# Chunked recurrence in seventeen steps, value sums on VectorE, and another split of the weight sums

## The chip, the cores and the metric

The kernel runs on one core of a Trainium2 chip. The metric is the device time of one execution in microseconds, the median of several runs. One execution was also profiled; its rows say how long each engine worked and what it waited for. The engines are TensorE (PE in the rows; PEld are its weight loads), VectorE (DVE), ScalarE (ACT), GpSimd (POOL) and SyncE (SP); SP and POOL issue the DMAs.

## The reference, cut to what matters

The reference is a trunk of two layers on 1024 rows of 1024 numbers, all float32. Layer 0 mixes rows with a gated linear recurrence of eight heads of 128 columns, layer 1 with a convolution module; each is followed by a squared-ReLU MLP of width 4096 and by layer normalisations. What the change touches is the recurrence and, through their weights, the value projection and the second matrices of both MLPs:

```python
proj = h @ w_in                       # columns [q | forget | value | output gate]
f = lb + (1 - lb) * sigmoid(fz);  k = 1 - f;  log_f = log(max(f, 1e-6))
...
def step(S, inp):                     # chunks of C rows, b = cumsum of log f within a chunk
    scores = einsum('bhtd,bhsd,bhtsd->bhts', qc, kc, decay)
    o = einsum('bhts,bhsv->bhtv', scores, vc) + einsum('bhtd,bhdv->bhtv', qc * exp(bc), S)
    S = exp(b_last) * S + einsum('bhsd,bhsv->bhdv', kc * exp(b_last - bc), vc)
...
o = o * rsqrt(mean(o^2) + 1e-6) * norm_g * silu(g);  mix = o @ w_out
...
ff = square(relu(x @ ffn_w1)) @ ffn_w2
```

## The kernel before, in words

**Products.** Every matrix product is split by a scheme of seven products over the four quadrants of its operands (numbered 1 to 7) in place of eight, and every operand is cut into two reduced-precision parts: ScalarE casts the high part and VectorE subtracts it for the low part (`cut`), and three multiplications stand for one. Products 5, 6 and 7 need sums of quadrants, which have to be made before they are cut. Products 1, 5 and 6 are copied out of PSUM by ScalarE, and later products are added to or subtracted from these copies (`v_out`).

**The value projection** is the first stage. `v_products(i, jobs)` issues product i in four pieces of 12 multiplications, and behind each piece its output copy, one job of the list and a tick of a clock that counts products. The order is 1, 2, 5, 6, 7, 3, 4. The inputs' quadrants (`x00`, `x01` ...) are combined on VectorE. Of the weights' quadrants a0 to a3, VectorE makes a2 + a3 (product 5) and a0 + a2 + a3 (product 6). The sums a0 + a2 (product 7) and a0 + a1 + a2 + a3 (product 3) are made in DRAM by `value_sums`: SP copies a0 and a1 into a DRAM tile `vsum`, POOL's DMAs add a2 and a3 and then the one half to the other, and `sum_v` loads both sums on SP.

**The pairs' stage.** Twelve pairs (a head's query and forget columns, or the output gates of two heads) follow, with seven products each of 12 multiplications. Between them the recurrences of the heads are woven in. `recurrence(h)` is a generator, and each `yield` ends a step. `slot()` is called at every third multiplication (four times in a product); each time `pace` is added to a sum, and a step is taken when it reaches one. Two heads may be under way together: the next starts when the first is at step `LAG`, and the steps alternate so that the lead stays near `LAG`. A head goes like this:

- On VectorE, F is written from the forget gate, `total(n)` multiplies neighbouring decay factors to products over 2n rows, and `scale(n)` multiplies queries and keys of blocks of n rows by them (n = 1, 2, 4 ... 64). `qk`, `T` and `F` in the rows are these.
- On TensorE, score products for blocks of 8 rows, the 4-wide ones (from `kd`, through a reciprocal), and those for 16, 32 and 64 write `level_ps`, two PSUM banks. `put(1)`, `put(0)` and `put(2)` copy them by mask (a predicated copy on VectorE) into the score buffer A (`at`), of which there are two, used in turn.
- Keys are transposed on TensorE and copied by ScalarE (`kt`).
- Then come eight chunks of 128 rows, one in a step. Each has a score product with the values and, but for the first, a product of the queries with the state; up to the seventh it also has a state product (`kt` with the values) into one PSUM slot, out of which VectorE writes the new state, decayed, into one of two buffers. After the fourth and the eighth chunk `settle` normalises half of the result into the head's F tile, and `give` transposes it, scales it and stores it by SP (`od <- f`). F has one buffer.

That makes 22 steps in a head. The gating with the output gates follows by loads and stores of its own (`gate_out`).

**Sums for the MLPs' second matrices.** `block_sums` makes, for one of 8 blocks of each of the two layers, the sums of weight quadrants in DRAM: two copies of 1 MB on SP and three accumulating DMAs on POOL, spread over ticks when a gap is given. There are 16 sets. Ten are issued in the pairs' stage (one in every eight products, not in the last pair), four in the first MLP's up stage, behind its blocks 1, 3, 5 and 7 counted from 0, and two in the convolution module.

**The rest.** Output projection and normalisation, first MLP up (`x1f`, `fw` in the rows) and down (`dw`, `dh`), convolution module, second MLP. No line of these differs but for the place of the sums.

**Who sets the order.** The instructions of TensorE, POOL and SP run in the order of the program text. Those of VectorE and ScalarE do so only until the end of the value projection; after that, a planner that simulates the kernel sets their order when it is built (a helper records most instructions, so that the rows show its line L173). An engine takes its instructions in order, so one that waits holds all behind it.

Of the kernel before, what the change touches and what calls it, by code (L numbers as in the profile page):

```python
# [15 lines left out]
P = 128  # L16
# [3 lines left out]
H = 8  # L20
# [217 lines left out]
def body(ctx, tc, d, out):  # L238
# [24 lines left out]
    def run(kb, n, size):  # L263
        return [kb + i * size for i in range(n)]
# [82 lines left out]
    x00, x10, x01, x11, t6 = [view(kb, (4, HT), F32, "xr") for kb in run(112, 5, 8)]  # L347
    a0, a1, a2, a3, s7 = [view(kb, (2, 1024), F32, "vr") for kb in run(152, 5, 8)]
    vd = [[dram.tile([P, NTB, HT], F32, name=f"vd{m}{n}") for n in range(2)] for m in range(2)]
# [15 lines left out]

    def value_sums(t, w, gap):

        def flat(x):
            return x.rearrange("a p n -> p a n")

        nc.sync.dma_start(out=flat(t), in_=flat(w)[:, 0:2])
        later(gap, lambda: nc.gpsimd.dma_start(out=flat(t), in_=flat(w)[:, 2:4], accum_op=ALU.add))
        later(2 * gap, lambda: nc.gpsimd.dma_start(out=flat(t)[:, 1], in_=flat(t)[:, 0], accum_op=ALU.add, max_dma_last_dim=4096))

# [101 lines left out]
    nc.sync.dma_start(out=par, in_=d["par"])  # L476
    vsum = dram.tile([2, 2, P, 1024], F32, name="vsum")
    for j in range(2):
        value_sums(vsum[:, j], d["wv"][:, j], 4)
    make_identity(nc, ident)  # L480
# [12 lines left out]
    def sum_v(out, i):  # L493
        for j in range(2):
            nc.sync.dma_start(out=out[:, j], in_=vsum[i, j])

# [11 lines left out]
    for k in range(4):  # L508
        if k < 3:
            diff(x00, x00, x01, (k + 1,))  # L510
        cut_x(5, x00, (k,))
    add_v(a2, a2, a3)
    for t in range(NTB):
        v_out(1, t)
    cut_v(5, a2)

# [11 lines left out]

    v_products(2, [lambda: x6(0, 1), lambda: x6(2, 3), lambda: add_v(a0, a2, a0), lambda: cut_v(6, a0)])
    outs_v(5)  # L530
    assert not waiting
    sum_v(s7, 0)
    sum_v(a1, 1)
    lg = par[:, LB : LB + H]
# [11 lines left out]

    v_products(5, [lambda: x7(0, 1), lambda: x7(2, 3)])
    cut_v(7, s7)
    x4(0, 1, 2, 3)
# [42 lines left out]
    level_ps, out_ps = (banks[:, k : k + 2].rearrange("p k (a b) -> p (k a) b", b=P) for k in (3, 5))  # L592
    state_ps = banks[:, 7, :P]
    count = {"at": 0}
    qk, gates, vts = {}, {}, {}
# [12 lines left out]
    def recurrence(h):  # L608
# [35 lines left out]
        yield  # L644
        scale(1)
        grow(2)
        yield
# [9 lines left out]
        yield  # L657
        A = at_[count["at"] % 2]
        count["at"] += 1
        levels(K, Q)  # L660
# [55 lines left out]
        if h == H - 1:  # L716
            assert (h - 1, 1) in done
            load_values(2 * h + 1, F[:, HT:].rearrange("p (a b) -> p a b", a=NTB))
        for c in range(2 * NTB):
            vc = vts[2 * h + c // NTB][:, c % NTB]  # L720
            if state is None:
                tensor.matmul(out_ps[:, c, :], A[:, c, :], vc, start=True, stop=True)
            else:
                tensor.matmul(out_ps[:, c, :], A[:, c, :], vc, start=True, stop=False)
                tensor.matmul(out_ps[:, c, :], Q[:, c * P : (c + 1) * P], state, start=False, stop=True)
            if c < nk:
                tensor.matmul(state_ps, kt[:, c, :], vc, start=True, stop=True)
                new = p1("state")
                if state is None:
# [12 lines left out]
        yield  # L742
        give(1)
# [63 lines left out]
    recs, active, done, pace, alone = [], [], set(), [0.0, 0.0], [False]  # L807
    LAG = 12

# [65 lines left out]
    def tail(i):  # L875
        if i == 6:
            wb_raw.append(raws((112, 116)))
            wb.ahead(1)
        elif i == 5:
            oT.extend([half_x(0, "oT"), half_x(32, "oT")])  # L880
        elif i == 7:
            assert not any(a[0] == H - 2 and a[2] < 21 for a in active)
            wb.ahead(3)
            back.append(ring(run(64, 8, 2), wide_t, "back"))
            assert len(stored) == 2 * H - 4
            gated(0, range(H - 2))
        elif i == 3:
            for half in range(2):
                u, g = back[0](), gates.pop((H - 2, half))
                nc.sync.dma_start(out=u, in_=od[H - 2][half])  # L890
                mul(u, u, g)
                into(half, H - 2, u)
        elif i == 4:
            wb.ahead(4)
            wa_raw.append(raws((80, 84)))
            wa.ahead(4)
# [7 lines left out]
    for _ in range(5):  # L904
# [8 lines left out]
        {  # L913
            "qk": ((2, 2 * HT), 3), "kd": ((2, 2 * HT), 1), "at": (chunks, 2), "f": (two_t, 1), "T": (two_t, 1), "kt": (chunks, 1), "t": (wide_t, 4),
            "sq": (wide_t, 2), "u": (wide_t, 2), "mask": ((3, P), 1), "rt": ((2 * P,), 1), "state": ((P,), 2), "dec": ((2 * NTB,), 2),
        },
    )
    vs = ring((124, 126), rows, "v")
    mask = p1("mask")
    at_ = [p1("at") for _ in range(2)]  # L920
    nc.sync.dma_start(out=mask, in_=d["mask"])
    for t in at_:
        nc.gpsimd.memset(t, 0.0)
# [381 lines left out]
    for c in range(NFC):  # L1305
        for i in ORDER[2 if c < 2 else 0 :]:
# [341 lines left out]
```

## Time and profile before

| | us |
|---|---|
| three runs | 2181.7, 2185.71, 2176.25 |
| median | 2181.7 |
| profiled execution | 2177.8 |
| its span in the profile | 2176.0 |
| TensorE busy in it (97%) | 2101.8 |
| VectorE busy (66%) | 1443.3 |
| ScalarE busy (48%) | 1040.8 |
| GpSimd busy (17%) | 380.7 |

The span runs from the first to the last recorded instruction; 1.8 us of the execution lie outside it. Over the span the DMA engines moved 515.95 MB, 237 GB/s in the mean, and the mean granted clock of TensorE was 0.992 of full speed. In the rows of waits, `X a L1 <- Y b L2: t, n, m` says that engine X, about to write a, waited for engine Y's work on b: t us in all, n times, the longest m. In the rows of the timeline a line is a run of like instructions: start, duration, engine, line, operation, out <- in, and in brackets how long the engine stood before it and for whom. In the rows of windows the columns are the window, its length, the engine's busy time with the number of instructions, the granted clock (behind TensorE's column alone, or behind all engines'), the DMA engines' busy share and GB/s.

### The profile page before, as it was taken

The page shows a single profiled execution, that of the slowest core. Times are in us where ns is not written, and L with a number is a line of the kernel's source. Part 1 is how long each engine was busy: PE and PEld are TensorE (multiplying, and loading weights), DVE is VectorE, ACT ScalarE, POOL GpSimd, SP SyncE. Part 2 cuts the span into 40 slices and gives each one's busy share as a digit, 9 for nine tenths or more (in the row PEclk, how much of TensorE's full clock was granted, in tenths as well). Part 3 has the DMA queues.
Part 4 walks back from the last instruction along what each step waited for, and adds up shares of the span by engine and source line. Part 5 has one row for each costly group of instructions (what it writes and reads, how often), then busy time and mean ns, then how long its engine had stood idle before and what let it go on. Part 6 is the DMA issues. An engine that isn't in the chain of part 4 may idle for free.

```text
span 2176.0 us, 27188 instructions
## 1 busy us (share of the span) xinstructions
PE 2101.8 (97%) x10056; PEld 1739.6 (80%) x10056; DVE 1443.3 (66%) x1886; ACT 1040.8 (48%) x1599; POOL 380.7 (17%) x349
## 2 busy tenths in 40 slices
PE   8889998999999999999999999999999999999998
PEld 6777776777888877878888888888878888888887
DVE  7587777867776665655566699789727444554446
ACT  4445454443255554634444577558552443443333
POOL 0001111111100000100001399279311000000002
PEclk9999999999999999999999999999999999999999
DMA  9566766676249988998998855665495888866652
GB/s 284 173 144 169 214 159 190 170 191 230 81 141 320 300 307 268 322 406 301 341 334 307 324 200 193 218 228 184 152 296 220 313 325 312 315 197 196 193 165 100
DMA packets 176318, 515.95 MB, mean 237 GB/s; under 512 B 16697, under 2 KB 45625, under 8 KB 175161
## 3 DMA queue, kind: packets, MB, share of 16 engines
q1 hardware_dynamic: 166392, 477.52, 62.0%
q0 software_dynamic: 9792, 36.70, 9.4%
q8 instruction: 78, 1.28, 0.2%
q14 instruction: 56, 0.45, 0.1%
HBM read 384.66 MB, written 201.85 MB: 270 GB/s over the span
## 4 chain that ended last, share of the span: by engine, by line
PE 71%; DMA 13%; DVE 7%; issue 3%; ACT 3%; POOL 3%; SPq 0%; DVEq 0%; POOLq 0%; ACTq 0%
PE ps L173 71%; POOL cb L173 2%; DMA next<-in_wpw_dram 2%; DVE qk L173 2%; DMA dh<-hf 1%; DMA wa<-ready 1%; DMA vsum<-in_wv_dram 1%; DMA hf<-ht 1%; DMA od<-f 1%; DMA y<-kept 1%; DMA hf<-hr 1%; DVE at L173 1%; DMA raw<-in_w1q_dram 1%; DVE fs L173 0%; DMA ready<-spare 0%
## 5 line engine op out<-in xcount | busy, mean ns | idle before, releaser
L173 PE MATMUL ps<-dw,dh 128*128 128x512 f32 x2688 | 612.9, 390 | 4.7 <-ACT dh L70 4.1
L173 PEld LDWEIGHTS ps<-dw,dh 128*128 128x128 f32 x2688 | 505.4, 188 | 110.2 <-ACT dh L70 4.6
L173 PE MATMUL ps<-x1f,fw 128*128 128x512 f32 x1344 | 309.7, 391 | 7.8 <-ACT c L1151 6.1
L173 PEld LDWEIGHTS ps<-x1f,fw 128*128 128x128 f32 x1344 | 251.1, 188 | 62.1 <-ACT c L1151 8.4
L173 PE MATMUL ps<-xa,wa 128*128 128x512 f32 x1152 | 268.8, 392 | 0.0
L173 PE MATMUL ps<-xf,fs 128*128 128x512 f32 x1008 | 265.7, 407 | 0.0
L173 PEld LDWEIGHTS ps<-xa,wa 128*128 128x128 f32 x1152 | 214.3, 188 | 43.3
L173 POOL TENSOR_TENSOR cb<-cb,prod 128x512 f32<-128x512 f32 x176 | 234.3, 1340 | 15.6 <-ACT prod L1416 4.7
L173 DVE TENSOR_TENSOR dw<-dr,dw 128x1024 fp32r<-128x1024 f32 x112 | 136.6, 1223 | 124.8 <-ACT dw L70 124.4
L173 DVE TENSOR_TENSOR dh<-dh 128x1024 fp32r<-128x1024 f32 x112 | 136.6, 1223 | 112.5 <-ACT dh L70 112.5
L173 PEld LDWEIGHTS ps<-xf,fs 128*128 128x128 f32 x1008 | 183.3, 191 | 34.3
L173 DVE SCALAR_TENSOR_TENSOR ps<-u,par,ps 128x512 f32<-128x512 f32 x288 | 199.1, 750 | 11.7 <-ACT ps L1428 10.2
L70 ACT CAST dh<-dh 128x1024 fp32r<-128x1024 f32 x112 | 117.1, 1050 | 150.0 <-DMA dh<-hf 149.2
L70 ACT CAST dw<-dr 128x1024 fp32r<-128x1024 f32 x112 | 117.4, 1052 | 141.4 <-PE ps L173 123.1
L173 PE MATMUL ps<-xc,wa 128*128 128x512 f32 x768 | 174.4, 389 | 0.0
L173 PEld LDWEIGHTS ps<-xc,wa 128*128 128x128 f32 x768 | 144.1, 188 | 29.8
L487 POOL TENSOR_TENSOR mv<-mv,nhalf 128x1 f32<-128x1 f32 x32 | 46.5, 1453 | 675.9 <-DVE mv L173 675.9
L1416 ACT ACTIVATE prod<-u,par 128x512 f32<-128x512 f32 x176 | 126.3, 723 | 61.6 <-POOL cb L173 60.3
L173 DVE TENSOR_TENSOR wa<-raw,wa 128x1024 fp32r<-128x1024 f32 x55 | 71.4, 1299 | 71.8 <-ACT wa L70 71.7
L70 ACT CAST wa<-raw 128x1024 fp32r<-128x1024 f32 x55 | 57.7, 1050 | 121.7 <-PE ps L173 106.0
L173 PE MATMUL ps<-vw,xf 128*128 128x512 f32 x336 | 82.5, 410 | 13.9 <-ACT vo L438 8.6
L1279 POOL COPY next<-ss 128x1 f32<-128x1 f32 x37 | 18.9, 510 | 414.3 <-DVE spare L173 271.6
(198 smaller groups left out, 2692.1 us busy)
## 6 DMA issues: line engine op xcount, KB each, us to landing
wa<-ready SPq DMA_DIRECT2D x122, 512.0 KB, 4.7
dh<-hf SPq DMA_DIRECT2D x112, 512.0 KB, 4.2
ready<-spare SPq DMA_DIRECT2D x74, 512.0 KB, 5.6
sum_w<-in_w_dram SPq DMA_DIRECT2D x32, 1024.0 KB, 7.5
dr<-sum_w SPq DMA_DIRECT2D x64, 512.0 KB, 4.7
raw<-in_w_dram SPq DMA_DIRECT2D x51, 512.0 KB, 5.5
dr<-in_w_dram SPq DMA_DIRECT2D x48, 512.0 KB, 6.4
raw<-in_w1q_dram SPq DMA_DIRECT2D x36, 512.0 KB, 5.1
```

The source lines that it names most:

```text
L70: self.nc.scalar.copy(out=slot[:, 0, c], in_=raw[:, c])
L173: return op(*args, **kw)
L487: nc.gpsimd.tensor_tensor(out=dst, in0=src, in1=nhalf[:, :n], op=ALU.pow)
L1279: nc.gpsimd.tensor_copy(out=raw[:, :1], in_=now)
L1416: nc.scalar.activation(tp, u[:, k : k + HT], AF.Copy, scale=tap(j, k))
```

## The change

**Value sums.** `value_sums`, `sum_v` and the DRAM tile go. VectorE makes all sums: s5 = a2 + a3 (product 5), s5 + a0 (product 6), a2 + a0 (product 7) and a1 + s5 (product 3), the last two as jobs behind the third and fourth piece of product 5. a2 is kept for that, and the fifth buffer holds s5 in place of the loaded sum.

**The recurrence** has 17 steps in place of 22. `scale(1)` and `grow(2)` become two steps. The state bank has four slots; `outer` issues the state products of four (then three) chunks together with the state updates behind them, and `attend` issues the products of four chunks with scores and states. One step holds `outer` of chunks 0 to 3, one `attend` of 0 to 3 with `outer` of 4 to 6, one `attend` of 4 to 7, then one `give` each. There are eight state buffers in place of two, and one score buffer in place of two. `LAG` is 9 instead of 12, and `pace` 0.54 and 0.5 instead of 0.74 and 0.66.

**Sums for the second matrices.** One set comes in every six products in the pairs' stage until four are left, which makes twelve; two come in the first up stage, behind blocks 0 and 2; two in the convolution module, as before.

```diff
-    a0, a1, a2, a3, s7 = [view(kb, (2, 1024), F32, "vr") for kb in run(152, 5, 8)]
+    a0, a1, a2, a3, s5 = [view(kb, (2, 1024), F32, "vr") for kb in run(152, 5, 8)]
-    def value_sums(t, w, gap):
...
-    vsum = dram.tile([2, 2, P, 1024], F32, name="vsum")
-    for j in range(2):
-        value_sums(vsum[:, j], d["wv"][:, j], 4)
...
-    add_v(a2, a2, a3)
+    add_v(s5, a2, a3)
     for t in range(NTB):
         v_out(1, t)
-    cut_v(5, a2)
+    cut_v(5, s5)
...
-    v_products(2, [lambda: x6(0, 1), lambda: x6(2, 3), lambda: add_v(a0, a2, a0), lambda: cut_v(6, a0)])
+    v_products(2, [lambda: x6(0, 1), lambda: x6(2, 3), lambda: add_v(s5, s5, a0), lambda: cut_v(6, s5)])
     outs_v(5)
-    assert not waiting
-    sum_v(s7, 0)
-    sum_v(a1, 1)
...
-    v_products(5, [lambda: x7(0, 1), lambda: x7(2, 3)])
-    cut_v(7, s7)
+    v_products(5, [lambda: x7(0, 1), lambda: x7(2, 3), lambda: add_v(a2, a2, a0), lambda: add_v(a1, a1, s5)])
+    cut_v(7, a2)
...
-    state_ps = banks[:, 7, :P]
-    count = {"at": 0}
+    state_ps = banks[:, 7].rearrange("p (a b) -> p a b", b=P)
...
         scale(1)
+        yield
         grow(2)
...
-        A = at_[count["at"] % 2]
-        count["at"] += 1
...
-        for c in range(2 * NTB):
-            vc = vts[2 * h + c // NTB][:, c % NTB]
-            if state is None:
-                tensor.matmul(out_ps[:, c, :], A[:, c, :], vc, start=True, stop=True)
-            else:
-                tensor.matmul(out_ps[:, c, :], A[:, c, :], vc, start=True, stop=False)
-                tensor.matmul(out_ps[:, c, :], Q[:, c * P : (c + 1) * P], state, start=False, stop=True)
-            if c < nk:
-                tensor.matmul(state_ps, kt[:, c, :], vc, start=True, stop=True)
+        def outer(cs):
+            for c in cs:
+                tensor.matmul(state_ps[:, c % NTB], kt[:, c, :], values(c), start=True, stop=True)
+            for c in cs:
                 new = p1("state")
-                if state is None:
-                    vector.tensor_copy(out=new, in_=state_ps)
+                if c == 0:
+                    vector.tensor_copy(out=new, in_=state_ps[:, 0])
                 else:
-                    vector.scalar_tensor_tensor(out=new, in0=state, scalar=dec[:, c : c + 1], in1=state_ps, op0=ALU.mult, op1=ALU.add)
-                state = new
-            if c % NTB == NTB - 1:
-                settle(c // NTB)
-                if h < H - 2:
-                    load_values(2 * h + 2 + c // NTB)
-            if c == 6:
-                give(0)
-            yield
-        yield
+                    vector.scalar_tensor_tensor(out=new, in0=states[c], scalar=dec[:, c : c + 1], in1=state_ps[:, c % NTB], op0=ALU.mult, op1=ALU.add)
+                states.append(new)
+
+        def attend(cs):
+            for c in cs:
+                tensor.matmul(out_ps[:, c, :], A[:, c, :], values(c), start=True, stop=c == 0)
+                if c:
+                    tensor.matmul(out_ps[:, c, :], Q[:, c * P : (c + 1) * P], states[c], start=False, stop=True)
+
+        outer(range(NTB))
+        yield
+        attend(range(NTB))
+        outer(range(NTB, nk))
+        settle(0)
+        yield
+        attend(range(NTB, 2 * NTB))
+        settle(1)
+        if h < H - 2:
+            for half in range(2):
+                load_values(2 * h + 2 + half)
+        yield
+        give(0)
         yield
         give(1)
...
-    LAG = 12
+    LAG = 9
...
-            "qk": ((2, 2 * HT), 3), ..., "at": (chunks, 2), ..., "state": ((P,), 2), "dec": ((2 * NTB,), 2),
+            "qk": ((2, 2 * HT), 3), ..., "at": (chunks, 1), ..., "state": ((P,), 8), "dec": ((2 * NTB,), 2),
...
-        pace[1] = 0.0 if p == 0 else 0.74 if p < 3 else 0.66
+        pace[1] = 0.0 if p == 0 else 0.54 if p < 3 else 0.5
...
-            if (7 * p + ORDER.index(i)) % 8 == 1 and p < len(PAIRS) - 1:
+            if (7 * p + ORDER.index(i)) % 6 == 1 and len(to_sum) > 4:
                 block_sums(*to_sum.pop(0), gap=12)
...
-        if c in (1, 3, 5, 7):
+        if c in (0, 2):
             block_sums(*to_sum.pop(0), f[:2, 1, :1].bitcast(F32))
```

More of the change, by code (lines that the diff above doesn't have):

```diff
@@ L364, in tick @@
                 job()
-    def value_sums(t, w, gap):
[L368 to L373, printed above, removed]
     sums = {}
@@ L491, in add_v @@
             vector.tensor_tensor(out=out[:, j], in0=x[:, j], in1=y[:, j], op=ALU.add)
-    def sum_v(out, i):
-        for j in range(2):
-            nc.sync.dma_start(out=out[:, j], in_=vsum[i, j])
     def diff(out, x, y, ks):
@@ L716, in recurrence @@
         if h == H - 1:
-            assert (h - 1, 1) in done
             load_values(2 * h + 1, F[:, HT:].rearrange("p (a b) -> p a b", a=NTB))
-        for c in range(2 * NTB):
-            vc = vts[2 * h + c // NTB][:, c % NTB]
-            if state is None:
-                tensor.matmul(out_ps[:, c, :], A[:, c, :], vc, start=True, stop=True)
-            else:
-                tensor.matmul(out_ps[:, c, :], A[:, c, :], vc, start=True, stop=False)
-                tensor.matmul(out_ps[:, c, :], Q[:, c * P : (c + 1) * P], state, start=False, stop=True)
-            if c < nk:
-                tensor.matmul(state_ps, kt[:, c, :], vc, start=True, stop=True)
+        states = [None]
@@ L728, in recurrence, with values @@
+        def values(c):
+            return vts[2 * h + c // NTB][:, c % NTB]
+        def outer(cs):
+            for c in cs:
+                tensor.matmul(state_ps[:, c % NTB], kt[:, c, :], values(c), start=True, stop=True)
+            for c in cs:
                 new = p1("state")
-                if state is None:
-                    vector.tensor_copy(out=new, in_=state_ps)
-                else:
-                    vector.scalar_tensor_tensor(out=new, in0=state, scalar=dec[:, c : c + 1], in1=state_ps, op0=ALU.mult, op1=ALU.add)
@@ L881, in tail @@
         elif i == 7:
-            assert not any(a[0] == H - 2 and a[2] < 21 for a in active)
+            assert not any(a[0] == H - 2 and a[2] < 15 for a in active)
             wb.ahead(3)
@@ L913, in body @@
         {
-            "qk": ((2, 2 * HT), 3), "kd": ((2, 2 * HT), 1), "at": (chunks, 2), "f": (two_t, 1), "T": (two_t, 1), "kt": (chunks, 1), "t": (wide_t, 4),
-            "sq": (wide_t, 2), "u": (wide_t, 2), "mask": ((3, P), 1), "rt": ((2 * P,), 1), "state": ((P,), 2), "dec": ((2 * NTB,), 2),
+            "qk": ((2, 2 * HT), 3), "kd": ((2, 2 * HT), 1), "at": (chunks, 1), "f": (two_t, 1), "T": (two_t, 1), "kt": (chunks, 1), "t": (wide_t, 4),
+            "sq": (wide_t, 2), "u": (wide_t, 2), "mask": ((3, P), 1), "rt": ((2 * P,), 1), "state": ((P,), 8), "dec": ((2 * NTB,), 2),
         },
@@ L919, in body @@
     mask = p1("mask")
-    at_ = [p1("at") for _ in range(2)]
+    A = p1("at")
     nc.sync.dma_start(out=mask, in_=d["mask"])
-    for t in at_:
-        nc.gpsimd.memset(t, 0.0)
+    nc.gpsimd.memset(A, 0.0)
     for i in range(2):
```

## The prediction

> **What bounds the kernel now.** I read the page first, then TensorE's waits in two parts of the span, its clock in short windows, and the timeline around each long wait.
>
> ```profile
> span 2176.0 us, 27188 instructions
> PE 2101.8 (97%) x10056; PEld 1739.6 (80%) x10056; DVE 1443.3 (66%) x1886; ACT 1040.8 (48%) x1599; POOL 380.7 (17%) x349
> ```
>
> TensorE is busy 97% of the span and the change leaves its multiplications as they are. All that can be won or lost is in the 74 us in which it stands still, and in stretches at a lower clock. Where are they? The waits of TensorE in the first 620 us (total, times, longest):
>
> ```profile
> PE ps L173 <- DVE state L173: 14.5, 20, 1.4
> PE ps L173 <- DVE at L173: 11.8, 11, 6.9
> PE ps L173 <- ACT vo L438: 8.6, 1, 8.6
> PE ps L173 <- DVE qk L173: 5.9, 2, 5.3
> PE ps L173 <- ACT kt L690: 2.8, 1, 2.8
> ```
>
> and in the rest of the span:
>
> ```profile
> PE ps L173 <- ACT c L1151: 6.1, 4, 2.1
> PE ps L173 <- ACT dh L70: 4.1, 1, 4.1
> ```
>
> A long wait is paid twice, since the granted clock (the column behind the busy time) falls in it and stays low after it:
>
> ```profile
> 60.00:64.00 4.00, 3.03 (x7) 0.50 0.37 123
> 64.00:68.00 4.00, 4.00 (x14) 0.70 0.01 4
> ...
> 132.00:136.00 4.00, 3.67 (x17) 0.50 1.08 257
> 136.00:140.00 4.00, 3.71 (x18) 0.74 0.61 121
> ...
> 476.00:480.00 4.00, 4.00 (x15) 0.57 0.46 151
> ```
>
> Behind the wait of 8.6 us, 3.03 us at half clock and 4 us at 0.70 lose 1.5 + 1.2 = 2.7 us; behind the one of 5.3 us it is 1.8 + 1.0 = 2.9 us; behind the one of 2.8 us it is 4 x 0.43 = 1.7 us. So I add 2.7 us to any wait near 5 us. [...]
>
> **Values' weight sums on VectorE.** Now two sums go through DRAM, and what reads them is late (timeline):
>
> ```profile
> 35.46 2.35 DVE L173 TENSOR_TENSOR vr<-vr 128x1024 f32<-128x1024 f32 x2
> 45.29 1.30 DVE L173 TENSOR_TENSOR xf<-xr,xf 128x512 fp32r<-128x512 f32 x2
> 56.14 1.23 DVE L173 TENSOR_TENSOR vw<-vr,vw 128x1024 fp32r<-128x1024 f32 x1 [7.10 <-ACT vw L399]
> 57.28 2.49 DVE L173 SCALAR_TENSOR_TENSOR xr<-xr 128x512 f32<-128x512 f32 x4
> 60.97 9.20 PE L173 MATMUL ps<-vw,xf 128*128 128x512 f32 x28 [8.56 <-ACT vo L438]
> ```
>
> TensorE finishes its fourth value product at 60.97 - 8.56 = 52.4 and resumes at 60.97, because ScalarE's copies of that product are queued behind the cut of the loaded sum. The change removes the DRAM sums, their loads and a stop of SP's and POOL's queues on them, and adds four additions on VectorE: two pairs at 2.35 us, 4.7 us, right behind the form that ends at 46.6. So 46.6 + 4.7 = 51.3, cut of the sum 2.4 -> 53.7, where the old chain reached 57.3: everything behind comes 3.6 us sooner, TensorE at 57.4. VectorE is then the late one, not a transfer. The wait left is 5.0 us, near the 5.3 us that lost the clock, so I credit no clock: **-3.6 us**. Bounds: 0 (VectorE meets another late cast) and -6.3 (the clock holds as well).
>
> **Seventeen steps per head: the start.** Head 0 starts while VectorE is already loaded:
>
> ```profile
> 117.31 0.69 DVE L173 TENSOR_SCALAR f<-qk 128x1024 f32<-128x1024 f32 x1 [0.65 <-ACT qk L774]
> 131.06 1.22 DVE L173 TENSOR_TENSOR qk<-qk,T 128x1024 f32<-128x1024 f32 x1
> 132.33 3.49 PEld L173 LDWEIGHTS ps<-qk 128*128 128x128 f32 x16 [5.70 <-DVE qk L173]
> 100.00:120.00 20.00, 20.00 (x90) 16.58 (x89) 12.93 (x20) 12.01 (x19) 2.06 (x2) 1.00 0.89 262
> ```
>
> 90 multiplications in 20 us are 0.222 us each, 2.67 us for a product of twelve. Head 0's first score products now stand 11.75 products after the stage's start, in the changed order 13.5. TensorE would come to them 1.75 x 2.67 = 4.7 us later, at 131.7; VectorE's order up to the scaling they need is the same but for one operation of 0.6 us, so it is done at 132.9. A wait of 1.2 instead of 5.3 us, and the clock holds: 4.1 + 2.9 = **-7.0 us**. Bounds: -8.2 and -3 (the queue is later, the clock falls).
>
> **The state products.** Grouped rows of VectorE from 187 to 463 us, six heads:
>
> ```profile
> L173 DVE TENSOR_TENSOR qk<-qk,T 128x1024 f32<-128x1024 f32 x37 | 45.2, 1223 | 15.8 <-PE ps L173 15.8
> L173 DVE COPY_PREDICATED at<-mask,ps 128x1024 f32<-128x1024 int32 x18 | 24.2, 1343 | 3.5 <-PE ps L173 3.5
> L173 DVE SCALAR_TENSOR_TENSOR state<-state,dec,ps 128x128 f32<-128x128 f32 x36 | 12.3, 341 | 3.5 <-PE ps L173 3.4
> L173 DVE RECIPROCAL rt<-T 128x256 f32<-128x256 f32 x6 | 10.5, 1752 | 0.0
> ```
>
> No operation goes. Today TensorE asks for a new state at every chunk, 0.75 product after its state product, and stands 14.5 / 20 = 0.7 us each time, because such an update queues behind scalings of 1.2 us and a reciprocal of 1.75 us. In the change it asks a whole product (2.67 us) after four state products, and the four updates are 0.3 + 3 x 0.34 = 1.3 us: most of the 14.5 us goes.
>
> What is late next? The same VectorE work. In the built order of the changed kernel the next head's first operations stand among the scalings for 16, 32 and 64, and TensorE waits for each of these. I walk one head in that order:
>
> ```profile
> 272.30 1.95 PE L173 MATMUL ps<-qk 128*128 128x128 f32 x16
> ```
>
> Take 1.95 us for a head's 16 score products, 0.7 and 1.1 us for the small ones at 32 and 64; on VectorE 0.6 us for 512 columns (four in 2.49 us above), 1.18 us for 1024 (two in 2.35), 1.3 us for a copy. Time 0 is the start of the score products for 8. TensorE then does these, one product, the 4-wide ones (to 7.2), one product, the score products for 16 (to 11.8), half a product, and wants the scaling by 16 at 13.1. VectorE makes the second copy from 7.5 to 8.8, then by its order F, a product with F, a total, a scaling, a cut and a small total (0.6 + 1.18 + 0.6 + 1.18 + 0.6 + 0.3 = 4.5, to 13.3) and only then the scaling by 16: 14.4, 1.3 us late. TensorE goes on, 0.7 + 2.67, and wants the scaling by 32 at 17.8; in front of it stand a scaling, a sum, a small total and the reciprocal (1.18 + 0.6 + 0.2 + 1.7): 18.1 + 1.2 = 19.3, 1.5 us late. After 1.1 + 2.67 more TensorE wants the last copy at 23.1; two sums, a cut, the product with the reciprocal, a small total, the scaling by 64 and the copy (1.2 + 0.6 + 1.2 + 0.1 + 1.2 + 1.3 = 5.6) end at 24.9, 1.8 us late. Together 4.6 us. Behind that come casts and one scaling, about 5 us, before the four updates, and TensorE asks 2 products and 2 us later: no wait there. TensorE's groups between products start some tenths late today, which gives VectorE back about 1.5 us per head in the walk, so I put 3.1 us against (14.5 + (11.8 - 6.9) + (5.9 - 5.3)) / 7 = 2.9 us now: 7 x 0.2 = +1.4. Five groups less per head, an estimated 0.1 us each, give 0.5 x 7 = -3.5. I take **-2 us**. Bounds: +12 (the walk's 4.6 in all heads, nothing for the groups) and -14 (nothing takes the states' place).
>
> The single score buffer is no new wait: a head writes it two steps after the head before has read it for the last time.
>
> **The store of a head's result.** A head's F tile is free only when the store of the head before last has read it:
>
> ```profile
> 365.04 0.60 PE L173 MATMUL ps<-ident,f 128*128 128x128 f32 x4
> 366.45 0.33 SPq L713 DMA_DIRECT2D od<-f  x1
> 375.59 0.69 DVE L173 TENSOR_SCALAR f<-qk 128x1024 f32<-128x1024 f32 x1 [4.04 <-DMA od<-f]
> 378.67 1.75 PE L173 MATMUL ps<-ident,qk 128*128 128x128 f32 x7 [6.91 <-DVE at L173]
> ```
>
> This is the wait of 6.9 us: a store of 9 us held VectorE 4 us with the last predicated copy queued behind it, and with the clock it cost 9.5 us. In the changed order the write of F stands earlier, just behind the second predicated copy in four heads and ahead of it in two: wanted 4.7 to 6 us after the transposes, where it was wanted 6.7 us after. The six stores now took from 2.4 to 9.1 us. At the same times three are early enough and three hold VectorE 2 to 6 us; with one lost clock that is about 10 us, as now: **0 us**, bounds -9.5 and the second rival.
>
> **Second MLP's sums.** Two sets move from the next stage into this one. A set's transfers (KB each, us to landing) and the waits that stand beside the last two sets:
>
> ```profile
> sum_w<-in_w_dram SPq DMA_DIRECT2D x16, 1024.0 KB, 7.3
> sum_w<-sum_w POOLq DMA_DIRECT2D x18, 512.0 KB, 7.0
> sum_w<-in_w_dram POOLq DMA_DIRECT2D x8, 1024.0 KB, 11.1
> od<-f SPq DMA_DIRECT2D x14, 256.0 KB, 2.4
> ...
> 852.52 3.03 PE L173 MATMUL ps<-x1f,fw 128*128 128x512 f32 x12 [2.12 <-ACT c L1151]
> 857.31 51.98 PE L173 MATMUL ps<-x1f,fw 128*128 128x512 f32 x228 [1.76 <-ACT c L1151]
> 946.91 3.67 PE L173 MATMUL ps<-dw,dh 128*128 128x512 f32 x8 [4.14 <-ACT dh L70]
> 920.00:960.00 40.00, 35.86 (x152) 29.21 (x151) 20.19 (x21) 13.91 (x14) 2.55 (x4) 0.96 1.04 397
> ```
>
> In the changed order the later stage's sets follow its first and third block; those behind the sixth and eighth go. They hold the engines over 18 us each, just ahead of the waits of 2.1 + 1.8 and 4.1 us, the last with the DMA engines full (1.04) and a clock of 0.96 (1.6 us of 40). I let 8 of these 9.6 us go, and keep the earlier 2.8 us: **-8 us**; bounds 0 and -11. SP and POOL no longer pass these issues ahead of the residual's loads. In the first stage a set now comes every 6 products, about 28 us with the recurrence between them, and its accumulations take 11 + 7 us before the last can start: POOL keeps up. The end of that stage loses the last set's traffic, but the transposed keys' copy now stands behind three weight casts: I take 0, bounds +4 and -4.
>
> **Sum.** -3.6 - 7.0 - 2 + 0 - 8 + 0 = -20.6. The profiled execution took 2177.8 us (1.8 us lie outside the span); 2177.8 - 20.6 = **2157 us**. The median shown is 2181.7 of runs from 2176.25 to 2185.71, so the profiled run is an ordinary one.
>
> **Rivals.** *VectorE becomes the bound of the recurrence (0.2).* The walk's 4.6 us stand in all seven heads, 32 against 20 us now: -2 becomes +12, the time 2171, no change. For: the order, in which the late scalings stand behind work that nobody waits for yet. Against: the rows above show VectorE waiting 15.8 + 3.5 + 3.5 us for TensorE in six heads, which is slack.
>
> *The F write waits in every head (0.17; slower).* For: a third more sum traffic in the stage, an earlier F write, and a store of 9.1 us when accumulations are in flight. Then each of six heads waits about 4.5 us and loses 2.7 us of clock: 43 us against 10 now, +33, time 2190. It decides from about five heads on. Against: half of all fourteen stores land in 2.4 us or less. [...]
>
> *The sums were not the cause of the later waits (0.1).* Then 8 us stay: 2165, still faster by a little.
>
> **Chances.** 0.53 for the forecast. A measurement here can tell about 0.5%, 11 us, from no change. Forecast and third rival, less what their bounds put within 11 us, give faster 0.62; the first rival and that rest, same 0.2; the second, with the overlap of the first, slower 0.18. The lower bounds together are -6.3 - 8.2 - 14 - 9.5 - 11 - 4 = -53. The range runs from two thirds of the way between the sum and these, 2177.8 - 42 = 2136, to the second rival's time, 2190, above which half of that rival's chance lies.
>
> **What would show it.** Right: TensorE's wait near 52 us is about 5 us; none of over 2 us near 130; "<- DVE state" falls below 5 us; "<- ACT dh" is gone. Wrong: F's idle time behind the store in most heads, a total of "<- DVE qk" and "<- DVE at" over 30 us, or the waits at 850 and 945 unchanged.

## The result, and the profile after

The changed kernel takes 2172.1 us in the median of 20 runs (2167.7 to 2177.0) against 2179.2 us of the kernel before in the same number: a ratio of 0.9968, 95% interval 0.9959 to 0.9978. That is 7.1 us less; the prediction was 20.6 us less. The runs of one kernel lie up to 14 us apart, and more in the kernel before, so a profile, which shows one execution, can differ from the median by some us. The profiled execution has a span of 2172.5 us. The page's first lines, and then TensorE's waits in three parts of the span (to 100 us, 100 to 620, from 620):

```profile
span 2172.5 us, 27149 instructions
PE 2103.5 (97%) x10056; PEld 1747.4 (80%) x10056; DVE 1451.1 (67%) x1890; ACT 1043.4 (48%) x1599; POOL 369.0 (17%) x344
```

```profile
PE ps L173 <- ACT vo L429: 3.9, 1, 3.9
...
PE ps L173 <- DVE qk L173: 25.7, 11, 6.0
PE ps L173 <- DVE at L173: 18.2, 7, 5.5
PE ps L173 <- DVE state L173: 2.3, 3, 1.3
PE ps L173 <- ACT kt L669: 1.3, 1, 1.3
...
PE ps L173 <- DMA wa<-ready: 2.1, 1, 2.1
PE ps L173 <- DVE c L173: 0.8, 1, 0.8
```

Three of the long rows of before are gone or small: the output copy of the value products (8.6 to 3.9), the state (14.5 to 2.3), and the waits of the up and down stages for ScalarE (10.2 to none). In their place the rows for the scalings (qk) and the predicated copies (at) went from 17.7 to 43.9 us.

Where the time went shows in windows cut at the stages' own ends: the pairs' stage and the first up stage, before and then after (the columns are window, length, five engines' busy time, granted clock, DMA share, GB/s):

```profile
96.30:492.20 395.90, 360.54 (x2246) 301.33 (x2245) 295.14 (x454) 178.34 (x406) 48.34 (x45) 0.98 0.68 181
...
588.10:909.10 321.00, 313.25 (x1403) 257.65 (x1402) 206.54 (x251) 175.42 (x259) 15.86 (x24) 1.00 0.83 270
```

```profile
91.20:504.10 412.90, 365.37 (x2246) 309.24 (x2244) 302.21 (x464) 183.36 (x419) 50.39 (x52) 0.95 0.75 201
...
597.90:910.10 312.20, 311.37 (x1402) 258.00 (x1401) 212.17 (x256) 182.25 (x266) 14.31 (x24) 1.00 0.78 259
```

The value projection ends 5.1 us sooner, the up stage is 8.8 us shorter, the output projection 2.1 us and all behind the up stage some 4.5 us. The pairs' stage is 17.0 us longer. In it TensorE stands still 47.5 us instead of 35.4, and the mean clock is 0.95 instead of 0.98. A clock of 0.95 costs 0.05 x 412.9 = 21 us, one of 0.98 costs 8 us. So by this estimate waits and clock together cost 25 us more, and since the stage grew by 17 only, the rest of TensorE's work in it became some 8 us shorter.

What do the long waits of this stage come from? Three of VectorE's rows there name a transfer, and the first of F's four waits stands in the timeline like this:

```profile
DVE u L173 <- DMA u<-od: 11.8, 6, 5.9
DVE total L173 <- DMA pr<-in_wp_dram: 9.5, 3, 5.6
DVE f L173 <- DMA od<-f: 9.2, 4, 4.4
```

```profile
172.70 0.33 SPq L692 DMA_DIRECT2D od<-f  x1
...
176.45 0.60 SPq L374 DMA_DIRECT2D sum_w<-in_w_dram  x1
...
182.45 0.69 DVE L173 TENSOR_SCALAR f<-qk 128x1024 f32<-128x1024 f32 x1 [4.36 <-DMA od<-f]
...
188.27 1.07 PE L173 MATMUL ps<-qk 128*32 128x32 f32 x32 [5.95 <-DVE qk L173]
```

```profile
184.00:188.00 4.00, 0.00 (x0) 0.93 1.05 366
188.00:192.00 4.00, 3.73 (x38) 0.50 0.83 221
192.00:196.00 4.00, 4.00 (x25) 0.72 0.00 0
```

A store issued at 172.7 lets F be written only at 182.5, VectorE stands 4.4 us with the scalings queued behind, TensorE 6.0 us behind those; then the clock is 0.50 and 0.72 for 8 us. The DMA engines are full from 172 to 188 (1.04 to 1.06). Six waits for the load of a stored result (`u`) and three for a block of weights (`pr`) hold VectorE in the same way, 11.8 and 9.5 us in all.

### The profile page after: what moved, and what is told of

It is laid out like the page before. It is cut to its first block, busy times and chain, and to the rows that moved or that the text cites. A ratio compares the mean times of both kernels' runs of the same rounds, so it can differ in the third digit from the quotient of the medians.

```text
span 2172.5 us, 27149 instructions
## 1 busy us (share of the span) xinstructions
PE 2103.5 (97%) x10056; PEld 1747.4 (80%) x10056; DVE 1451.1 (67%) x1890; ACT 1043.4 (48%) x1599; POOL 369.0 (17%) x344
## 4 chain that ended last, share of the span: by engine, by line
PE 82%; DMA 6%; DVE 6%; POOL 3%; issue 1%; ACT 1%; SPq 0%; DVEq 0%; POOLq 0%; ACTq 0%
PE ps L173 82%; POOL cb L173 3%; DMA od<-f 2%; DVE qk L173 1%; DMA wa<-ready 1%; DMA raw<-in_w_dram 1%; DMA u<-od 1%; DMA pr<-in_wp_dram 1%; DMA vr<-in_wv_dram 1%; DVE at L173 0%; DVE vr L173 0%; DVE fs L173 0%; DVE xf L173 0%; DVE t L173 0%; ACT xf L390 0%
## 5 line engine op out<-in xcount | busy, mean ns | idle before, releaser
L173 PEld LDWEIGHTS ps<-xf,fs 128*128 128x128 f32 x1008 | 192.3, 198 | 38.6
L173 PE MATMUL ps<-xb,wa 128*128 128x512 f32 x384 | 89.3, 391 | 0.0
```

What stands on the lines that cost most here:

```text
L173: return op(*args, **kw)
```

## The experiments

Every ratio below is to the kernel before in runs beside it; a difference between two kernels is that of their medians. Those runs of the kernel before had medians of 2178.0 to 2180.9 us, so a difference across experiments is known to a few us at best. Two theories were set against each other. **Order:** with the new steps VectorE's early work of the next head stands ahead of the scalings that TensorE waits for. **Transfers:** the sums' traffic delays stores and loads that VectorE waits for, with those scalings queued behind.

**Ten sets in the stage.** The changed kernel with the sums as they were.

```diff
-            if (7 * p + ORDER.index(i)) % 6 == 1 and len(to_sum) > 4:
+            if (7 * p + ORDER.index(i)) % 8 == 1 and p < len(PAIRS) - 1:
...
-        if c in (0, 2):
+        if c in (1, 3, 5, 7):
```

> The changed kernel with the sums where they were: ten sets in the pairs' stage (one in every eight products), four in the first up stage, two later. Two theories of why the pairs' stage got 17 us longer (395.9 to 412.9 us). Order: VectorE, with the next head's first operations among the scalings that TensorE waits for, is late in every head; then the stage stays near 412 us, the waits of the up and down stages (10 us) come back, and the time is about 2182 us. Transfers: two more sets delay the stores and loads that VectorE waits for; then the stage falls to about 402 us, the 10 us come back later, and the time is about 2172 us, with TensorE's waits for qk and at together below 30 us instead of 43.9.

Measured: 2177.3 us, ratio 0.9990 (0.9973 to 1.0006); stage 406.4 us, qk and at 36.7 us; the waits of the up and down stages are back (4.7 for `dh`, 3.5 for `c`). Half way between the theories.

**Each small part alone.** Before with only the value sums, and before with only the sums' places.

> The kernel before with the value sums on VectorE alone. The wait near 52 us should fall from 8.6 to about 4 us, and the value projection end 5 us sooner (91 instead of 96 us). If that gain holds to the end: 2174 us against 2179. If the recurrence's start, for which VectorE is late anyway, gives it back: 2178.

> The kernel before with the sums' new places alone: twelve sets in the pairs' stage, two in the first up stage, two later. The up and down stages should lose their 10 us of waits. Order theory: the pairs' stage stays near 396 us, so 2169 us in all. Transfers theory: the stage grows by 8 to 10 us, to about 405, F's waits for its store come in most heads, and the time is about 2178 us.

Measured: 2173.7 us, 0.9980 (0.9962 to 0.9999); and 2163.8 us, 0.9931 (0.9909 to 0.9952). The value sums give 5.4 us (0.2 to 8 by the interval). The places alone give 15.4 us (10 to 20), more than the whole change; with the old recurrence the pairs' stage hardly minds two more sets (397.0 us).

**The old recurrence under the other two parts**, which leaves out the seventeen steps, `LAG`, `pace` and the buffers:

> The changed kernel with the old recurrence: before, with the value sums on VectorE and the sums' new places. If the parts add (-5.4 alone and -15.4 alone), 2158 us, and the recurrence's part in the changed kernel is +14. If the two parts' gains overlap, 2163 us, and it is +9.

Measured: 2157.4 us, 0.9902 (0.9878 to 0.9926). The two parts add to within 1 us, which is closer than either is known, and the new recurrence costs 14.7 us on top of them. With ten sets the same difference (the first kernel above against the value sums alone) is 3.5 us, and this one is not clear: the twelve runs of each reach from 2171.9 to 2183.2 and from 2168.3 to 2182.4 us, and in the two profiled executions the pairs' stages are 13 us apart (406.4 and 393.4).

**Another lead.** The next head starts later, by 12 or by 11 steps in place of 9.

```diff
-    LAG = 9
+    LAG = 12
...
-        pace[1] = 0.0 if p == 0 else 0.54 if p < 3 else 0.5
+        pace[1] = 0.0 if p == 0 else 0.74 if p < 3 else 0.66
```

> The changed kernel with the lead of 12 steps and the old pace (0.74, 0.66): the next head starts when all scalings of the one before are done. Order theory: TensorE's waits for qk and at fall from 43.9 to some 15 us, the pairs' stage from 413 to about 395, the time to about 2157 us. Transfers theory: the waits stay above 35 us, and the time within 5 us of 2172.

> The changed kernel with a lead of 11 steps, and the pace raised in proportion to the steps taken per head (22 against 18: 0.66, 0.61). The next head's first operations come only when the scalings of the one before are issued. Order theory: the waits for qk fall from 25.7 to about 7 us, those for at do not grow, the pairs' stage goes from 413 to about 402, the time to about 2161 us. Transfers theory: the sum of both waits stays above 38 us, the time within 4 us of 2172 or above.

Measured: 2183.7 us, 1.0021 (1.0005 to 1.0037), and 2195.1 us, 1.0076 (1.0051 to 1.0102): both worse. (With 12 steps a head's factors in F are overwritten by the result of the head before, so that its scalings are by other numbers.) The order theory is right about one row: qk falls from 25.7 to 6.7 and 8.1. But at rises to 33.1 and 47.2, and in the second kernel F waits 18.2 us for its store:

```profile
226.98 0.69 DVE L173 TENSOR_SCALAR f<-qk 128x1024 f32<-128x1024 f32 x1 [6.35 <-DMA od<-f]
...
228.72 1.30 DVE L173 COPY_PREDICATED at<-mask,ps 128x1024 f32<-128x1024 int32 x1
...
230.08 3.78 PE L173 MATMUL ps<-kd 128*128 128x128 f32 x16 [5.76 <-DVE at L173]
```

A predicated copy that TensorE needs now stands behind F.

**One transfer's wait away.** First the result is written over the head's dead keys, so that F waits for no store; then the product with the gates, which waits for the load, is made by GpSimd.

```diff
-        o, on = F.rearrange("p (a b) -> p a b", b=P), F
+        o, on = K.rearrange("p (a b) -> p a b", b=P), K
```

```diff
         def rest():
-            mul(u, u, g)
+            nc.gpsimd.tensor_tensor(out=u, in0=u, in1=g, op=ALU.mult)
```

> The changed kernel with a head's result written over its dead keys, so that F's next write waits for no store. Transfers theory: VectorE's 9.2 us of waits for the store go, with them TensorE's waits near 188 (6.0 us), 286 (3.6) and part of 377 (5.5) and the clock that they cost, so about 2160 us. Order theory: F is written sooner, and the operations behind it still stand ahead of the late scalings; the waits for qk and at stay above 35 of 43.9 us, and the time within 4 us of 2172.

> The changed kernel with the product with the output gates (u, 12 times 0.6 us of VectorE, and its 11.8 us of waits for the load of the stored result) on GpSimd. Transfers theory: TensorE's wait of 4.4 us near 228 and parts of those near 386 and 398 go, 8 to 12 us with the clock, so about 2162 us. Order theory: 7 us less work of VectorE in the stage takes some 3 us of the late scalings, so about 2169 us.

Measured: 2171.0 us, 0.9959 (0.9944 to 0.9975), and 2174.4 us, 0.9976 (0.9958 to 0.9995): next to nothing. In each the other waits grew: without F's store, VectorE's wait for `u` is 25.7 us instead of 11.8, and TensorE's for the state 15.9 instead of 2.3; without `u`, F's wait is 12.4 instead of 9.2 and the blocks' 15.7 instead of 9.5.

**Both away at once**, in the new and in the old recurrence:

> The changed kernel with the result over the dead keys and the gates' product on GpSimd: VectorE waits neither for the store of a result nor for its load (9.2 + 11.8 us in the changed kernel; each edit alone only moved the wait to the other). Transfers theory: TensorE's waits in the stage fall from 47 to about 25 us, with the clock 20 us in all: stage near 395, time near 2153 us. Order theory: the late scalings stay (qk 14 us), stage near 404, time 2163 to 2168 us.

> The old recurrence with value sums on VectorE, the sums' new places, the result over the dead keys, and the gates' product on GpSimd. VectorE's 12.6 us of waits for the load go; those of TensorE that hang on them were few (34 us of waits in all, 18 for the state). Transfers theory: 5 us, to 2152. Order theory: 0 to 3 us, 2155 to 2157.

Measured: 2158.0 us, 0.9905 (0.9887 to 0.9924), and 2152.8 us, 0.9873 (0.9855 to 0.9891). The new recurrence gains 14.1 us, the old one 4.7; the new is 5.3 us behind, with 19.5 us of VectorE's waits for blocks left. Its time lies half way between the two theories; its stage, 392.8 us in the fastest of its runs, is nearer to that of the transfers theory.

**No sums in the stage**, in both recurrences.

```diff
     def block_sums(name, layer, c, after=None, gap=0):
+        if gap:
+            sums[name, layer, c] = d[name][layer, c]
+            return
```

> The changed kernel without the twelve sets of sums in the pairs' stage; the second matrices' products that need sums read single quadrants instead. Its pair is the next run, the same with the old recurrence. Transfers theory: without the sums' traffic the new recurrence is as good as the old or better, stage near 388, the two kernels within 4 us. Order theory: the new one stays 10 us or more behind the old one, stage near 400, with waits for qk and at above 30 us.

> The old recurrence, value sums on VectorE, and the same twelve sets left out. Both theories: little comes of it, since F's waits were only 0.5 us with the old recurrence: stage about 390 us (397 with the sums), time about 2150 us.

Measured: 2147.1 us, 0.9846 (0.9828 to 0.9865), and 2151.8 us, 0.9870 (0.9852 to 0.9889). Here the new recurrence is the better one, by 4.7 us. TensorE's waits in the stage and the stage's window, new and then old:

```profile
PE ps L173 <- DVE qk L173: 18.8, 14, 2.7
PE ps L173 <- DVE at L173: 10.3, 10, 1.9
PE ps L173 <- DVE state L173: 3.0, 3, 1.3
...
89.60:475.00 385.40, 352.16 (x2244) 297.49 (x2243) 301.41 (x464) 183.49 (x419) 15.15 (x16) 0.99 0.27 85
```

```profile
PE ps L173 <- DVE state L173: 15.2, 20, 2.5
PE ps L173 <- DVE at L173: 7.6, 11, 2.7
PE ps L173 <- DVE qk L173: 5.3, 1, 5.3
...
91.30:479.40 388.10, 359.54 (x2246) 300.55 (x2245) 294.93 (x454) 178.31 (x405) 17.77 (x15) 0.98 0.25 79
```

The new recurrence still waits more (33.2 us against 28.6), and does the rest in less. Its waits are many and short, none over 2.7 us, and the mean clock stays at 0.99. The sums' traffic adds 412.9 - 385.4 = 27.5 us to its stage, and 397.1 - 388.1 = 9.0 us to that of the old one. With the traffic go most of VectorE's waits for transfers: in the new recurrence F's and those for blocks are gone and 4.1 us for `u` are left of 30.5 us in all, in the old one 8.3 of 21.4 us.

Leaving the sums out also takes their issues from SP's and POOL's queues. No run separates these from the traffic.

**Bursts or amount.** The changed kernel with the sums' transfers of 1 MB in halves, and with three of the sets issued in the value projection:

```diff
-        nc.sync.dma_start(out=v[:, 0:2], in_=w[:, 0:4:2])
-        later(gap // 2, lambda: nc.sync.dma_start(out=v[:, 2:4], in_=w[:, 0:2]))
-        parts = [lambda: nc.gpsimd.dma_start(out=v[:, 0:2], in_=w[:, 2:4], accum_op=ALU.add)]
+        for i, (o, j) in enumerate(((0, 0), (1, 2), (2, 0), (3, 1))):
+            later(i * gap // 4, lambda o=o, j=j: nc.sync.dma_start(out=v[:, o], in_=w[:, j]))
+        later(gap // 2, lambda: nc.gpsimd.dma_start(out=v[:, 0], in_=w[:, 2], accum_op=ALU.add, max_dma_last_dim=4096))
+        parts = [lambda: nc.gpsimd.dma_start(out=v[:, 1], in_=w[:, 3], accum_op=ALU.add, max_dma_last_dim=4096)]
```

```diff
+    block_sums(*to_sum.pop(0), gap=12)
     v_products(5, ...)
...
+    block_sums(*to_sum.pop(0), gap=12)
     v_products(7, ...)
+    block_sums(*to_sum.pop(0), gap=12)
     v_products(4, [make_form])
...
-            if (7 * p + ORDER.index(i)) % 6 == 1 and len(to_sum) > 4:
+            if (7 * p + ORDER.index(i)) % 8 == 1 and len(to_sum) > 4:
```

> The changed kernel with every transfer of 1 MB of a set in two of 512 KB, spread over the same time. If bursts delay the stores and loads, VectorE's waits for transfers fall from 30 to about 18 us and the time to about 2163 us; if the amount does, the time stays within 4 us of 2172.

> The changed kernel with three sets issued in the value projection and nine, one in every eight products, in the pairs' stage. If the amount matters: the pairs' stage falls from 413 to about 402 us (406 with ten sets), the value projection grows by at most 2 us, and the time is about 2161 us. If the new recurrence is late by itself: 2167 us or more.

> The changed kernel with the result over the dead keys, the gates' product on GpSimd and three sets early. Transfers theory: from 2158 to about 2150 us, level with or ahead of the next run. Order theory: 2156, and 3 us or more behind the next run.

> The old recurrence with value sums on VectorE, the result over the dead keys, the gates' product on GpSimd and three sets early. 2153 without the early sets; the stage had 13 us of waits of VectorE for block loads left and few of TensorE behind them: 2150 us.

Measured: 2177.5 us, 0.9986 (0.9970 to 1.0002), for the halves. The time tells nothing clear, for a reason in the timeline:

```profile
20.13 7.50 SPq L375 DMA_DIRECT2D sum_w<-in_w_dram  x7
...
53.35 1.14 ACT L391 CAST xf<-xr 128x512 fp32r<-128x512 f32 x2 [14.09 <-DMA vd<-vo]
...
68.28 34.46 PE L173 MATMUL ps<-vw,xf 128*128 128x512 f32 x144 [16.06 <-ACT vo L430]
```

Some copies of the four later sets no longer overlap the small write that holds them back. SP, like TensorE and POOL, keeps the order of the text only up to the end of the recurrences; the planner orders what comes behind, and it put these copies into the value projection; there a store of a value product kept ScalarE waiting 14 us. That stage ends at 102.4 instead of 90.9 us. The pairs' stage took 406.8 us (102.6 to 509.4) instead of 412.9, in one execution: bursts may be worth up to 6 us of the 27. But the row that the expectation named speaks against them: VectorE's waits for transfers in the stage are 30.8 us (14.9 for `u`, 10.4 for F, 5.5 for blocks) where it had 18 if bursts mattered.

The first of the kernels with early sets took 2176.3 us, 0.9977 (0.9960 to 0.9994); with both waits away 2161.7 us (0.9906, 0.9883 to 0.9929) and, old recurrence, 2158.2 us (0.9898, 0.9877 to 0.9918). All three were worse than without early sets, by 4.2, 3.7 and 5.4 us (the second within its noise), and the new recurrence is 3.5 us behind the old one, which is within the noise too. The gain that the transfers theory had in each did not come. But these runs do not test it: the last early set stood ahead of the loads of the first blocks, one of which made VectorE wait 14.7 us and TensorE 10.8, and the stage of the first is 415.4 us instead of 402.

**Two sets early**, ahead of the value products 5 and 6, ten in the stage, both waits away, new and old recurrence:

> The changed kernel with the result over the dead keys, the gates' product on GpSimd, two sets in the value projection and ten, one in every eight products, in the pairs' stage. The wait of 11 us at the head of the stage goes: 2151 us if the thinner traffic helps (2158 with twelve sets in the stage); level with the next run by the transfers theory, 4 us or more behind it by the order theory.

> The old recurrence with the same: 2150 us (2153 with twelve sets in the stage).

Measured: 2146.3 us, 0.9838 (0.9812 to 0.9864), and 2152.4 us, 0.9869 (0.9843 to 0.9896). The first is the fastest version of this study, and the new recurrence is ahead by 6.1 us; the runs of the two kernels do not overlap. Its stage:

```profile
PE ps L173 <- DVE qk L173: 12.1, 11, 2.4
PE ps L173 <- DVE at L173: 10.4, 10, 4.3
PE ps L173 <- DVE state L173: 8.4, 6, 2.2
...
92.00:475.50 383.50, 352.17 (x2246) 297.92 (x2244) 299.68 (x452) 183.07 (x419) 65.34 (x58) 0.99 0.72 194
```

## Why the prediction was wrong

That the kernel still became faster is in part luck, since the larger errors have opposite signs: the sums' places gave 15 to 16 us where 8 were forecast, and the recurrence cost 14.7 us where a gain of 9 was.

**Value sums: -3.6 forecast, -5.4 measured** for the part alone, within its bounds. The sum was cut at 52.3 (forecast 53.7), TensorE resumed at 55.98 (forecast 57.4), and the wait is 3.9 us (forecast 5.0). The clock still fell, as assumed (0.50 from 56 to 60 us, 0.86 in the next 4).

**The start of the first head: right in its mechanism.** The wait of 5.3 us before its score products is gone; they begin at 127.9 us without one. It stays, with 5.3 us, in the old recurrence under the same sums. No run has this part alone, so the 7 us are not shown.

**Second MLP's sums: -8 forecast, 15.4 and 16.3 us measured** (the places alone, and the same step on top of the value sums). With the places alone, the up stage takes 313.2 us (588.1 to 901.3) instead of 321.0, and what follows it 7.2 us less. I had kept 2.8 us of the earlier waits, but none of the waits for ScalarE is left, and what follows gained more than the wait of 4.1 and the clock of 1.6 that I saw there. The cause was right (with the old places the waits for ScalarE came back), the term too small by half and beyond its bound of -11.

**The recurrence: here the prediction failed.** Start, state products and store came to -7 - 2 + 0 = -9 us; the runs show +14.7. The step that failed is the store of a head's result, priced at 0 as the only transfer that counts. With the sums' traffic the new recurrence is 14.7 us behind the old one, without it 4.7 ahead: what the traffic costs it beyond the old one is some 19 us, where the sum has 0. Two sizes in the state products' step may have been off too, against each other.

- *The walk of VectorE's order was right, at its upper end.* It gave 4.6 us a head, 32 us in seven. Without the sums' traffic qk and at wait 18.8 + 10.3 = 29.1 us, and they stand where the walk has them: ahead of the score products for 32 and for 64, and behind the last copy. One head, where it gave 1.3, 1.5 and 1.8 us:

```profile
228.27 0.70 PE L173 MATMUL ps<-qk 128*32 128x32 f32 x32 [1.46 <-DVE qk L173]
...
233.15 1.15 PE L173 MATMUL ps<-qk 128*64 128x64 f32 x16 [1.23 <-DVE qk L173]
...
239.12 1.51 PE L173 MATMUL ps<-ident,qk 128*128 128x128 f32 x7 [1.88 <-DVE at L173]
```

(One of its sums is off: 1.95 + 2.67 + 1.95 is 6.6 and not 7.2; both engines' times behind it shift by the same, and the waits stay.) I took 3.1 a head, on the ground that TensorE gives time back. The first rival had the rows right (44 us measured, its mark was 30), but not the reason: by the order alone the new recurrence is still faster.

- *Fewer groups were perhaps worth more.* I put 0.1 us for each of 35, 3.5 us, an estimate for which the prediction names no row. The timeline of before bears out its size: runs of 3, 6 and 9 multiplications with `xf` that start at 156.54, 164.41 and 154.04 are followed by the next start after 0.78, 1.46 and 2.14 us, which is 0.68 for three and 0.10 for the run. The lost clock, added up over windows of 4 us for the time in which TensorE works, is 6.9 us before, 18.7 after, and without sums 4.1 in the new and 6.3 in the old recurrence. Without the waits and this, TensorE's own work in the stage is 353.7 us before and 346.7 after, and without sums 348.1 in the new and 353.2 in the old: 5 to 7 us less, from one execution each. That the number of groups is the cause was not tested.
- *Transfers were priced at 0, and for F's store alone.* F's wait did come in four heads, as the second rival's mechanism has it, yet its total is 9.2 us against 7.0. (What was held against that rival, half of all fourteen stores landing in 2.4 us or less, reads too much into the row: the trace records the landing of only seven of them.) With it came the load of the stored result (11.8 against 8.2) and the block loads (9.5 against 4.7), which no step priced. Taking F's wait away gave 1 us, since the others grew; taking two away gave 14 us, and the whole traffic 25 us (2172.1 to 2147.1) in the new recurrence against 6 us (2157.4 to 2151.8) in the old.

So the same traffic costs the new recurrence about three times as much in the stage, and some four times in the whole time. In the trace its scalings and copies stand behind the waiting operation and are late already; the stall is passed on to TensorE whole, as one wait of 4 to 6 us (VectorE's 4.4 us for F became TensorE's 6.0), and the clock is charged too (0.50 to 0.57 behind these waits). The old one has a state update of 0.34 us to wait for at each chunk, and with the sums it waits 17.9 us for it in 17 pieces. That this lack of slack is the cause is how I read the timeline; shown is the effect in the pairs of runs. It need not be all: with the same twelve sets the new recurrence's store takes 6.1 us in the median and the old one's 2.9 (2.0 in both without sums), and VectorE waits 30.5 against 21.4 us for transfers. Why its stores meet the sums more is open. Which of the waits decides was not separated beyond the pair taken away.

**The clock after a wait.** In the changed kernel the waits of 4.4 us (its end at 227.8) and 5.5 us (377.1), whose windows stand below, and that of 6.0 us above were followed by 0.50 to 0.57. The 2.8 us of the kernel before, followed by 0.57, are no lone exception among the shorter ones. In the changed kernel a wait of 2.8 us that ends at 244.6 is followed by 0.68 (244 to 248), one of 2.6 (389.1) by 0.60 and one of 3.1 (435.2) by 0.57. Without sums one of 2.7 (184.8) is followed by 0.67 (185.6 to 189.6), and even one of 1.9 (239.1) ends in a window of 0.73 (237.6 to 241.6). Another of 2.7 there (319.1) and one of 2.4 in the changed kernel (143.8) were followed by 1.00. So in these traces waits of 1.9 to 3.1 us can cost clock too, and a wait's length alone does not decide it.

```profile
228.00:232.00 4.00, 4.00 (x19) 0.57 1.05 336
...
378.00:382.00 4.00, 4.00 (x18) 0.50 0.05 12
...
388.00:392.00 4.00, 2.94 (x19) 0.60 1.04 179
436.00:440.00 4.00, 4.00 (x12) 0.57 0.88 235
```

## What to carry to other kernels

A change of the order on one engine can be worth its price in an empty kernel and lose in the real one (here 4.7 us ahead without the sums' traffic, 14.7 behind with it): price it together with every transfer that this engine waits for, loads too, and ask for each what is queued behind. Several such waits can cover one another, as here (1 us for one taken away, 14 for two), so taking one away can show nothing; take all that share a place away before the theory is dropped. Where background traffic is moved, look at the loads that it is put ahead of.

## What the runs showed that was not expected

The small transfers of the stage depend on the sums. A result's store, a load of it and a block's load of 256 KB each (columns: queue, operation, times, KB each, median us to landing), in the changed kernel with the sums, and without:

```profile
od<-f SPq DMA_DIRECT2D x14, 256.0 KB, 6.1
u<-od SPq DMA_DIRECT2D x12, 256.0 KB, 3.5
pr<-in_wp_dram SPq DMA_DIRECT2D x43, 256.0 KB, 5.1
```

```profile
od<-f SPq DMA_DIRECT2D x14, 256.0 KB, 2.0
u<-od SPq DMA_DIRECT2D x12, 256.0 KB, 3.0
pr<-in_wp_dram SPq DMA_DIRECT2D x43, 256.0 KB, 2.8
```

The mean share of the DMA engines was 0.75 with the sums, so they were not full on average; the medians were three times as long for the store and nearly twice for the blocks all the same, and hardly longer for the load. Each is the median of those transfers alone whose landing the trace records, 5 to 6 of the stores and loads and 18 to 20 of the blocks' loads. In the old recurrence with the same sums the store's median is 2.9 us.
